# A streaming encoder step with SSD, GLA and RWKV-7 branches: weight splits in a thread, a third token-copy buffer, later transposes and gating, and new charges in the emitter

## The chip, the cores and the metric

The kernel runs on one core of a Trainium2 chip. The metric is the device time of one execution in microseconds. The engines are TensorE (PE; its weight loads are listed as PEld), VectorE (DVE), ScalarE (ACT), GpSimd (POOL) and SyncE (SP), whose queue issues nearly all DMA transfers. Each engine works off its instructions in the order in which they stand in the program; what another engine or a transfer must finish first is waited for there, with everything behind it.

## The reference

One step of a hybrid encoder layer on 544 frames (512 of a prompt and 32 of a running stream), model width 1024, and 256 memory tokens. Cut to what matters:

```python
proj = u @ w_in                      # u = RMSNorm(h); one projection for all three branches
xbc = silu(conv4(xbc)); o_ssd  = gated_rmsnorm(ssd(xs, dt, A, B, C), z)   # 16 heads x 64, state 128
glog = log_sigmoid(low_rank(u)); o_gla = head_rmsnorm(gla(q, k, v, glog)) * silu(ggate)  # 4 heads, 128 x 256
o_rwkv = (head_layernorm(rwkv7_scan(r, w, k, v, kk, a)) + bonus) * silu(rgate)           # 16 heads x 64
m = s0 * (o_ssd @ P_ssd) + s1 * (o_gla @ P_gla) + s2 * (o_rwkv @ P_rwkv)  # s = sigmoid(merge gates of u)
h = h + m @ w_out
h = h + cross_attention(RMSNorm(h), K, V)   # K, V = RMSNorm(mem) @ wk, @ wv; 4 heads x 256
y = RMSNorm(h)
```

All of it is in f32. The three recurrences are written frame by frame in the reference; the kernel evaluates them in chunks of 64 or 128 frames. In RWKV-7 a chunk needs the inverse of a unit lower-triangular 64 x 64 matrix for each head. The outputs are y, the final states of the three recurrences and the memory's K and V.

## The kernel before, in words

**Dense work.** All weights lie in DRAM as blocks of 128 output columns (128 x 1024 with the eight k-blocks side by side). A block is loaded into a tile `wraw` and split into a high part `wh` (a rounding copy on ACT) and a low part `wl` (a subtraction on DVE); the activations are split in the same way (`uh`, `ul`). A block is then multiplied in two halves of 272 frames (256 for the memory), each by 24 products into one PSUM bank `pd`: alternately uh·wh and ul·wh for the eight k-blocks, then eight times uh·wl. The page counts 4896 of these products with u and streamed blocks, and 1152 with u and blocks that stay resident (`wr`); those of the memory, the projections and the attention come on top. `wh` and `wl` have two buffers each, `wraw` two or three.

**RWKV part.** The 16 heads go as eight pairs p. For each pair, `rw_A` prepares decays and keys, stores token-major copies (tiles `tm` and t8, the latter shown as t in the profile, both from the ring `tm`; the copies go to `NK` by DMA) and forms the triangular matrices, which go to DRAM (`n_scr`). `rw_I` loads them (`nd`) and solves the diagonal 32 x 32 blocks on POOL by 31 steps of two instructions (`im`, `td`; 62 in all), then stores the inverses (`d_scr`). `rw_J` loads these into `TT`, transposes one block on DVE (x1, shown as x), and completes the inverse with two groups of small products, W and T. `rw_C` is the chain over nine chunks: a product into `pc`, the sum `R` on DVE, a product with TT, then the new state `Sb`. The solve of the next pair runs beside the chain of the current one.

**The other threads.** `start_mem` and `start_x` norm the memory and the frames at the start (column sums `pss`, then `rsm` by a logarithm and an exponential on ACT); GLA and SSD threads run beside and behind the RWKV part; `gated` and `ssd_norm` load each branch's output and gate tiles (`yt`, `gt`) back from DRAM, gate them and split them as inputs of the projections.

**What sets the order.** The whole program is written out by a small scheduler (`Sched`) when it is built. It keeps a modelled clock for each engine, and charges each instruction a modelled duration. Each part above is a Python generator, a thread with a priority; where it yields a number, it is taken up again when PE's modelled clock has advanced by that much, and `S.at(x)` is the time until x is written by the model. The dense work is the thread of lowest priority (`dense`, 9): it fills PE whenever no other thread is due, and yields after every five products. The low part of a split is a thread of priority -1, which is above all others. So a charge in the model that is changed deals out the instructions of all engines anew. On the chip the model has no part: there the fixed orders meet the real durations.

**Names and lines.** A dense product is recorded at L245, an ACT activation at L278, a DVE or POOL instruction of two tensors at L284, a DMA at L327, the transposes of TT at L1122. The high part's copy is issued in `split_w`, before the thread `low` is added; `dense` picks the next block (`more`) before a block's first product. In the model a POOL instruction in `tt` costs 2.1 ns an element and 230 ns.

Of the kernel before, what the change touches and what calls it, by code (L numbers as in the profile page):

```python
# [11 lines left out]
AF = mybir.ActivationFunctionType  # L12
# [34 lines left out]
       ("a", "v"): 145.0, ("a", "p"): 170.0, ("v", "a"): 130.0, ("v", "p"): 155.0, ("p", "v"): 70.0, ("p", "a"): 65.0,  # L47
       ("a", "q"): 150.0, ("v", "q"): 150.0, ("p", "q"): 150.0, ("v", "v"): 127.0, ("a", "a"): 153.0, ("p", "p"): 102.0}

W = dict(HOLD1=0, HOLD2=8, CALM=3000, EARLY1=1, DEPTH1=3, EARLY2=2, FAIR=1500, GRAIN=5, IS=900.0, IE=0, NQ=3000, XL=2, SG=6, PRW=800.0, R2=0.0, DE=2500.0, T2=0, FA=900.0, XM=3000.0, WARM=12, KM=1500.0)  # L50


class Cols:
# [72 lines left out]
class Sched:  # L126
# [22 lines left out]
    def run(self):  # L149
        idle = 0  # L150
        while self.threads:
# [4 lines left out]
            th = next(ready, None)  # L156
            if th is not None and th[0] >= 0 and self.n_small > W["FAIR"]:
                th = next((x for x in ready if x[0] == 9), th)
# [78 lines left out]
    def mm(self, out, lhsT, rhs, start, stop, transpose=False, shared=False):  # L237

        n = rhs.free_size()
        k, m = lhsT.partition_size(), lhsT.free_size()  # L240
        if transpose:
            self.nc.tensor.transpose(out, lhsT, rhs)  # L242
            ns = 107.0 if k > 64 else 40.0
        else:
            self.nc.tensor.matmul(out, lhsT, rhs, start=start, stop=stop, skip_group_check=shared)  # L245
            if lhsT.dtype == F32R:
                ns = n / 2.4 + 12.7
            elif m <= 64:
                ns = max(60.0, n * 0.95 + 14)
            else:  # L250
                ns = max(107.0, n * 1.67)
        small = k < 128 or m < 128
        if self.small and not small:
            ns += 150
        elif small and not self.small:
            ns += 90
        self.small = small
        self.n_small = self.n_small + ns if lhsT.dtype != F32R else 0.0
        if start:
            self.note("pe", ns, (out,), (lhsT, rhs))  # L260
        else:
            self.note("pe", ns, (), (lhsT, rhs))
            self.mark(out, 0, "pe", self.t["pe"])
# [76 lines left out]
def body(tc, I, O):  # L340
    nc = tc.nc
    S = Sched(nc)
# [17 lines left out]
    with tc.manual_schedule(), \  # L360
# [104 lines left out]
        raw, spl, splitting = {}, {}, set()  # L465
        wn = [0]
        n_late = [0]
        ahead = []
        look = {"depth": W["DEPTH1"], "early": W["EARLY1"]}

        def ready(j):
            return j.get("cond") is None or j["cond"]()
# [16 lines left out]
        def split_w(j):  # L489
            blk = j["blk"]  # L490
            if blk in spl or blk in splitting:
                return
            tag, w = raw.pop(blk)
            if "res" in j:
                h, l = (pools["res"][1].tile([128, 1088], F32R, name="wr", tag=t) for t in j["res"])
            else:
                k = wn[0] % 2
                wn[0] += 1
                h, l = (base.tile([128, 1088], F32R, name=n_, tag=f"{n_}{k}") for n_ in ("wh", "wl"))
            h, l = h[:, :1024], l[:, :1024]  # L500
            S.act(h, w, AF.Copy)
            hl = tuple(a.rearrange("p (a b) -> p a b", b=128) for a in (h, l))

            def low():
                yield S.at(h)
                S.tt(l, w, f32(h), SUB)
                free_raw[tag] = S.since(w, 1)
                done.add(f"split {blk}")
                spl[blk] = hl

            splitting.add(blk)
            S.add(low(), -1)
# [31 lines left out]
        def dense():  # L544

            nxt = []

            def more(n):
                j = take() if len(nxt) < n else None
                if j is not None:  # L550
                    nxt.append(j)

            while True:
                commit()
                more(1)
                if not nxt:
                    presplit()
                    if not ahead and "end" in done:
                        return
                    yield lambda: any(ready(j) for j in ahead) or (commit() or any(ready(j) for j in ahead)) or "end" in done  # L560
                    continue
                cur = nxt.pop(0)
                commit()
                more(1)
                presplit()
                yield lambda: cur["blk"] in spl
                h, l = spl[cur["blk"]]
                if "res" not in cur:
                    del spl[cur["blk"]]
                    splitting.discard(cur["blk"])  # L570
                x = cur["x"]
                m = cur.get("m", 128)
                hv = cur.get("hv", ((0,) + HV[0], (1,) + HV[1]))
                if "late" in cur:
                    yield lambda: n_late[0] < 3
                    n_late[0] += 1
                for hi, o, w in hv:
                    ps = pd.tile([128, 512], F32, name="pd", tag="pd")
                    yield max(S.at(h), S.since(ps, 1) - S.t["pe"])
                    c = 0  # L580
                    for kb, part in [(kb, part) for kb in range(8) for part in (0, 1)] + [(kb, 2) for kb in range(8)]:
                        if c == 16:
                            yield S.at(l)
                        a = l if part == 2 else h
                        S.mm(ps[:m, :w], a[:, kb, :m], x(kb, o, w)[part % 2], start=c == 0, stop=c == 23)
                        c += 1
                        if c % W["GRAIN"] == 0 and c < 24:
                            commit()
                            yield None
                    if hi == hv[-1][0] and W["T2"]:  # L590
                        commit()
                        more(2)
                    if "late" in cur:
                        S.add(late(cur, ps), -0.5)
                        continue
                    if "ucond" in cur:
                        yield cur["ucond"]
                    cur["use"](hi, ps)
                    done.add(f"{cur['blk']}:{hi}")
                    yield None  # L600
                done.add(cur["blk"])
# [288 lines left out]
            return a.rearrange("p (c t) -> p c t", t=64)  # L890

        HP = ((0, 288), (288, 288))
        TMB = 2

        def rw_A(p):

# [214 lines left out]
        def rw_J(p):  # L1111

            yield has(f"rwJ{p}")
            rwr = pools["rwR"][1]
            d = slot[p % NSLOT]
            nk, tt_ = d["NK"], d["TT"]
            for h in range(2):
                S.dma(out=tt_[h * 64:h * 64 + 64, :, h * 64:h * 64 + 64], in_=rows64(d_scr, h))
            yield S.at(tt_)
            x1 = rwr.tile([128, 8, 32], F32, name="x1", tag="xw")  # L1120
            for h in (0, 64):
                nc.vector.transpose(x1[h:h + 64], tt_[h:h + 64, 0:8, h:h + 32])  # L1122
                S.note("v", 340, (x1[h:h + 64],), (tt_[h:h + 64],))
            yield S.at(x1) + W["XM"]
            ps = yield from bank("pW")
            for c in range(8):
                for h in (0, 64):
                    S.mm(ps[h:h + 64, c * 32:c * 32 + 32], nk[h:h + 32, c, h // 64, h // 32, :], x1[h:h + 32, c, :], True, True)
            w = rwr.tile([128, 8, 32], F32, name="W", tag="xw")
            S.act(w.rearrange("p c j -> p (c j)"), ps[:, :256], AF.Copy)  # L1130
            yield S.at(w)
            ps = yield from bank("pT")
            for c in range(8):
                for h in (0, 64):
                    S.mm(ps[h:h + 32, c * 32:c * 32 + 32], w[h + 32:h + 64, c, :], tt_[h + 32:h + 64, c, h + 32:h + 64], True, True)
            for h in (0, 64):
                S.act(tt_[h:h + 32, 0:8, h + 32:h + 64], ps[h:h + 32, :256].rearrange("p (c t) -> p c t", t=32), AF.Copy)
            done.add(f"rwI{p}")
            yield None

        IE = "pv"[W["IE"]]
# [534 lines left out]
        def gated(br, t):  # L1676

            yield has(*[f"{dict(rwkv='rg', gla='gg')[br]}{j}" for j in range(8)])
            low = None
            for j, (yt, gt) in enumerate(gate_loads(br)):  # L1680
                yield S.at(yt, gt)
                S.stt(yt, yt, 0.5, gt, MUL, MUL)
                if low:
                    low()
                low = split_o(br, t, j, yt)
                yield S.free("v")
            low()
            done.add(f"O{br}")

        def ssd_norm(t):  # L1690
# [2 lines left out]
            yield has(*[f"z{j}" for j in range(8)])  # L1693
            ys, rr = [], []
            for j, (yt, gt) in enumerate(gate_loads("ssd")):
                yield S.at(yt, gt)
                S.stt(yt, yt, 0.5, gt, MUL, MUL)
                if j % 4 == 0:
                    sq = gp.tile([128, T], F32, name="nsq", tag="nsq")
# [423 lines left out]
```

## Time and profile before

| | before |
|---|---|
| median of 3 runs (lowest to highest) | 1303.99 us (1301.09 to 1306.32) |
| profiled execution, its own time | 1301.87 us |
| its span in the trace | 1300.1 us |
| PE busy | 1260.5 us, 97% |
| DVE busy | 838.8 us, 65% |
| ACT busy | 627.3 us, 48% |
| POOL busy | 361.6 us, 28% |
| mean granted TensorE clock | 0.99 of full speed |

The profile is of one execution. Busy time counts the instructions of an engine; PE's products are pipelined, so its busy time holds overlaps and is not work at its peak. The granted clock is a share of TensorE's full 2.4 GHz. In a timeline a row gives the start, the duration, the engine, the line, the operation with the tile that it writes and the tiles that it reads, and in brackets the idle time of the engine before it and what ended that.

### The profile page before, as it was taken

How to read it: one execution, taken by the hardware profiler on the slowest of the kernel's cores; microseconds unless marked ns; L12 is line 12 of the kernel's file. 1: busy time of each engine (PE TensorE's matmuls, PEld its weight loads, DVE VectorE, ACT ScalarE, POOL GpSimd, SP SyncE). 2: the span in 40 equal slices, each digit the busy share in tenths (PEclk: the TensorE clock that was granted, in tenths of full speed). 3: DMA queues.
4: the chain of work that ended last, by engine and by line, in shares of the span. 5: the costliest groups of instructions: out<-in, count | busy, mean ns of one | idle time of the engine just before them, and what ended most of it. 6: DMA issues, size and time to landing. Idle time of an engine off the chain costs nothing.

```text
span 1300.1 us, 27497 instructions
## 1 busy us (share of the span) xinstructions
PE 1260.5 (97%) x10848; PEld 1215.3 (93%) x10848; DVE 838.8 (65%) x1666; ACT 627.3 (48%) x1191; POOL 361.6 (28%) x706
## 2 busy tenths in 40 slices
PE   8999989999999999999999999989999999999997
PEld 8999989999998999999999999978999999999997
DVE  6857747675858586844456586877665846575543
ACT  6664534557373637444364646364444423544422
POOL 0012837375656645551001062432100000000000
PEclk8999989999999999999999999999999999999999
DMA  8644462727363635364253243343887445540302
GB/s 291 190 129 111 131 147 64 182 75 183 84 167 96 156 96 151 99 174 134 101 191 114 76 127 109 103 135 114 277 311 251 141 144 181 171 146 25 106 17 70
DMA packets 170385, 181.11 MB, mean 139 GB/s; under 512 B 100480, under 2 KB 123104, under 8 KB 170128
## 3 DMA queue, kind: packets, MB, share of 16 engines
q1 hardware_dynamic: 169824, 178.68, 45.1%
q8 instruction: 86, 1.41, 0.5%
q10 hardware_dynamic: 432, 0.67, 0.2%
q14 instruction: 43, 0.35, 0.1%
HBM read 136.27 MB, written 35.39 MB: 132 GB/s over the span
## 4 chain that ended last, share of the span: by engine, by line
PE 54%; DVE 7%; ACT 2%; issue 1%; POOL 1%; DMA 0%; POOLq 0%; DVEq 0%; ACTq 0%; SPq 0%
PE pd L245 42%; PE pc L245 2%; PE psc L245 1%; PE pov L245 1%; PE py L245 1%; PE pO L245 1%; DVE wl L284 1%; DVE acc L293 1%; PE ph L245 1%; DVE AR L284 1%; PE pT L242 1%; PE pss L245 1%; PE pS L245 0%; DVE seg L299 0%; PE pp L245 0%
## 5 line engine op out<-in xcount | busy, mean ns | idle before, releaser
L245 PE MATMUL pd<-ul,wh 128*128 128x272 f32 (+1 forms) x1632 | 434.5, 295 | 0.0
L245 PE MATMUL pd<-uh,wh 128*128 128x272 f32 (+1 forms) x1632 | 431.1, 294 | 3.1 <-ACT wh L278 2.3
L245 PEld LDWEIGHTS pd<-uh,wh 128*128 128x128 f32 (+1 forms) x1632 | 307.1, 188 | 6.9 <-ACT wh L278 2.8
L245 PEld LDWEIGHTS pd<-ul,wh 128*128 128x128 f32 (+1 forms) x1632 | 307.4, 188 | 3.0 <-issue 1.5
L245 PE MATMUL pd<-uh,wl 128*128 128x272 f32 (+1 forms) x1632 | 251.4, 291 | 0.0
L245 PEld LDWEIGHTS pd<-uh,wl 128*128 128x128 f32 (+1 forms) x1632 | 219.9, 188 | 2.7 <-issue 1.4
L284 DVE TENSOR_TENSOR wl<-wraw,wh 128x1024 fp32r<-128x1024 f32 (+1 forms) x143 | 182.2, 1277 | 29.7 <-ACT wh L278 28.2
L278 ACT ACTIVATE wh<-wraw 128x1024 fp32r<-128x1024 f32 (+1 forms) x143 | 149.3, 1047 | 44.9 <-PE pd L245 27.4
L284 POOL TENSOR_TENSOR im<-td,nd 108x84 f32<-108x84 f32 (+23 forms) x248 | 110.8, 447 | 176.4 <-DMA td<-in_eye 86.5
L245 PE MATMUL pd<-uh,wr 128*128 128x256 f32 (+1 forms) x768 | 148.6, 291 | 1.4 <-ACT uh L278 1.4
L245 PEld LDWEIGHTS pd<-uh,wr 128*128 128x128 f32 x768 | 121.0, 188 | 3.0 <-ACT uh L278 1.6
L284 POOL TENSOR_TENSOR td<-td,im 108x84 f32<-108x84 f32 (+23 forms) x248 | 117.5, 474 | 19.4
L284 POOL TENSOR_TENSOR macc<-macc,hrs 128x288 f32<-128x288 f32 x3 | 2.3, 792 | 372.6 <-DVE macc L293 372.6
L245 PE MATMUL pd<-ul,wr 128*128 128x256 f32 (+1 forms) x384 | 100.2, 292 | 0.1
L245 PEld LDWEIGHTS pd<-ul,wr 128*128 128x128 f32 x384 | 72.4, 188 | 1.0 <-issue 0.4
L278 ACT ACTIVATE lerpA<-pd,par 128x272 f32<-128x272 f32 x50 | 24.4, 487 | 71.1 <-PE pd L245 60.2
L278 ACT ACTIVATE fg<-pd 128x272 f32<-128x272 f32 x64 | 25.3, 397 | 66.2 <-PE pd L245 56.0
L293 DVE SCALAR_TENSOR_TENSOR Sb<-Sb,GC,pc 64x64 f32<-64x64 f32 x128 | 35.7, 279 | 32.3 <-PE pc L245 30.3
L278 ACT ACTIVATE NK<-pc 128x128 f32<-128x128 f32 x136 | 30.5, 275 | 46.3 <-DVE Sb L293 44.5
L278 ACT ACT_TABLE_LOAD x39 | 50.0, 1283 | 3.9 <-DVE tB L284 1.6
L293 DVE SCALAR_TENSOR_TENSOR fg<-fg,pd 128x272 f32<-128x272 f32 x48 | 20.7, 433 | 47.5 <-ACT fg L278 47.2
L278 ACT ACTIVATE fg<-pd,dpar 128x272 f32<-128x272 f32 x48 | 23.3, 486 | 51.0 <-PE pd L245 46.6
(469 smaller groups left out, 2461.1 us busy)
## 6 DMA issues: line engine op xcount, KB each, us to landing
wraw<-in_wall SPq DMA_DIRECT2D x165, 512.0 KB
g_mg<-fg SPq DMA_DIRECT2D x24, 272.0 KB
mgt<-g_mg SPq DMA_DIRECT2D x24, 272.0 KB
NK<-tm SPq DMA_DIRECT2D x96, 64.0 KB
ab<-acs_d SPq DMA_DIRECT2D x8, 512.0 KB
nd<-n_scr SPq DMA_DIRECT2D x24, 144.0 KB
n_scr<-NK SPq DMA_DIRECT2D x16, 144.0 KB
TT<-d_scr SPq DMA_DIRECT2D x16, 144.0 KB
```

The lines of the kernel that those rows point to most:

```text
L242: self.nc.tensor.transpose(out, lhsT, rhs)
L245: self.nc.tensor.matmul(out, lhsT, rhs, start=start, stop=stop, skip_group_check=shared)
L278: self.nc.scalar.activation(out=out, in_=in_, func=f, scale=scale, bias=bias)
L284: eng.tensor_tensor(out=out, in0=a, in1=b, op=op)
L293: self.nc.vector.scalar_tensor_tensor(out=out, in0=a, scalar=s, in1=b, op0=op0, op1=op1)
```

## The change

Six edits:

1. `split_w`: the ACT copy of the high part is issued inside the thread `low`, once the raw block has landed by the model; before, it was issued at once, when the block was picked.
2. `dense`: after every five products, if no next block is picked, the first block of the list `ahead` is picked when it can start and its raw weights have landed by the model (or are being split already).
3. The ring `tm` has three buffers instead of two.
4. `rw_J`: the transposes of `TT` are issued 1500 ns of modelled time later.
5. `gated` for GLA, and `ssd_norm`: each tile's gating is issued 2000 ns of modelled time later.
6. The model's charge for an f32 product with more than 64 output rows rises from max(107, 1.67 n) to max(220, 1.79 n) ns, n being its columns.

```diff
-W = dict(HOLD1=0, ..., KM=1500.0)
+W = dict(HOLD1=0, ..., KM=1500.0, TM=1500.0, GM=2000.0)
...
             else:
-                ns = max(107.0, n * 1.67)
+                ns = max(220.0, n * 1.79)
...
             h, l = h[:, :1024], l[:, :1024]
-            S.act(h, w, AF.Copy)
             hl = tuple(a.rearrange("p (a b) -> p a b", b=128) for a in (h, l))
 
             def low():
+                yield S.at(w)
+                S.act(h, w, AF.Copy)
                 yield S.at(h)
                 S.tt(l, w, f32(h), SUB)
...
                         if c % W["GRAIN"] == 0 and c < 24:
                             commit()
+                            if not nxt and any(ready(j) and (j["blk"] in spl or j["blk"] in splitting or S.at(raw[j["blk"]][1]) == 0.0) for j in ahead[:1]):
+                                more(1)
                             yield None
...
-        TMB = 2
+        TMB = 3
...
-            yield S.at(tt_)
+            yield S.at(tt_) + W["TM"]
...
-                yield S.at(yt, gt)
+                yield S.at(yt, gt) + (W["GM"] if br == "gla" else 0.0)
...
-                yield S.at(yt, gt)
+                yield S.at(yt, gt) + W["GM"]
```

At the start, on ACT: the squares (`NK`) of the memory tokens, the weights' high parts and the reciprocal norm `rsm`, in the kernel before:

```order
L278 ACTIVATE wh<-wraw 128x1024
L278 ACTIVATE NK_124<-mem 128x256 x7
L278 ACTIVATE wh<-wraw 128x1024
L278 ACTIVATE NK_124<-mem 128x256
L278 ACTIVATE wh<-wraw 128x1024 x2
L278 ACTIVATE rsm<-pss,col 128x256
L278 ACTIVATE rsm<-rsm 128x256
```

and in the changed one, the same place:

```order
L278 ACTIVATE NK_124<-mem 128x256 x2
L278 ACTIVATE wh<-wraw 128x1024
L278 ACTIVATE NK_124<-mem 128x256 x6
L278 ACTIVATE wh<-wraw 128x1024 x2
L278 ACTIVATE rsm<-pss,col 128x256
L278 ACTIVATE rsm<-rsm 128x256
L278 ACTIVATE NK_124<-AR_119 128x544
L278 ACTIVATE wh<-wraw 128x1024
```

The first block of 128 x 1024 here is the second of the program, so the fifth block's copy, which stood directly ahead of `rsm`, now stands behind it. On PE the column sums `pss` for it come after 63 dense products in the changed program and after 72 before.

On SP, the DMA queue, at the drain of the second solve and the feed of the third (`d_scr` and `TT` are the drain, `n_scr`, `nd` and `td` the feed), in the kernel before:

```order
L327 DMA d_scr<-td 36x11x32
L327 DMA d_scr<-td 36x10x32
L327 DMA d_scr<-td 36x11x32
L327 DMA TT_125<-d_scr 64x9x64 x2
L327 DMA wraw<-in_wall 128x1024
L327 DMA NK_1070<-tm 64x4x64 x4
L327 DMA g_rwkv<-fg 128x544
L327 DMA wraw<-in_wall 128x1024
L327 DMA n_scr_140<-NK_1070 64x9x64 x2
L327 DMA nd<-n_scr_140 36x32x32 x3
L327 DMA td<-in_eye 108x352
```

and in the changed one:

```order
L327 DMA w2r<-in_w2a 128x256
L327 DMA d_scr<-td 36x11x32
L327 DMA d_scr<-td 36x10x32
L327 DMA d_scr<-td 36x11x32
L327 DMA TT_125<-d_scr 64x9x64 x2
L327 DMA nd<-n_scr_140 36x32x32 x3
L327 DMA wraw<-in_wall 128x1024
L327 DMA td<-in_eye 108x352
```

The matrices of the next pair (`n_scr`) are stored before the drain now, and their load `nd` follows TT directly, with one weight block between it and `td`. At the next three drains `n_scr` follows TT directly.

On PE, in the RWKV part, the eight groups of W products (one for each pair) have 312, 302, 303, 336, 316, 341 and 322 dense products between one and the next before, 2232 in all; in the changed program 283, 207, 259, 249, 279, 289 and 306, which is 1872. The RWKV part's end comes after 3298 dense products instead of 3701.

Behind it, on PE, GLA's third head (transposes `pT`, gates `pgk`, states `pS`) beside SSD (`pxt`, `py`), in the kernel before:

```order
L245 MATMUL pA_10952<-g_qe_8886,g_ke 32x32
L242 MATMUL pxt<-con,xs_8860 32x128
L242 MATMUL pxt<-con,xs_8861 32x128
L242 MATMUL pxt<-con,xs_8862 32x128
L242 MATMUL pxt<-con,xs_8863 32x128
L242 MATMUL pT<-con,g_gl 128x128 x4
L242 MATMUL pT<-con,gvf 128x128 x8
L242 MATMUL pT<-con,gvf 32x128 x2
L242 MATMUL pT<-con,g_gl 32x128
L245 MATMUL pgk<-smt,gw_8871 128x272 x2
L245 MATMUL pS<-vt,kt 128x256
```

and in the changed one:

```order
L245 MATMUL pd<-uh,wh 128x272
L245 MATMUL pd<-ul,wh 128x272
L242 MATMUL pT<-con,g_gl 128x128 x4
L242 MATMUL pT<-con,gvf 128x128 x8
L242 MATMUL pT<-con,gvf 32x128 x2
L242 MATMUL pT<-con,g_gl 32x128
L245 MATMUL pd<-uh,wh 128x272
L245 MATMUL pd<-ul,wh 128x272
L245 MATMUL pd<-uh,wh 128x272
L245 MATMUL pd<-ul,wh 128x272
L245 MATMUL pd<-uh,wh 128x272
L245 MATMUL py<-seg,xc 64x128 x8
```

Dense products (`pd`) stand here ahead of the transposes and between them and `py` now, where none stood.

## Rows read from the trace of the kernel before

**Rows 1.** The page, busy time and share of each engine with its instructions.

```profile
PE 1260.5 (97%) x10848; PEld 1215.3 (93%) x10848; DVE 838.8 (65%) x1666; ACT 627.3 (48%) x1191; POOL 361.6 (28%) x706
```

**Rows 2.** Windows; us, then PE, PEld, DVE, ACT, POOL busy, PEclk, DMA, GB/s.

```profile
21.50:25.90 4.40, 4.38 (x24) 4.38 (x25) 3.91 (x15) 2.57 (x6) 0.00 (x0) 0.61 0.73 209
174.70:609.20 434.50, 420.48 (x4077) 404.49 (x4076) 289.51 (x610) 224.47 (x463) 236.76 (x498) 0.99 0.48 130
188.10:193.20 5.10, 4.92 (x21) 4.60 (x21) 2.63 (x7) 1.92 (x7) 4.41 (x16) 0.50 0.97 259
845.00:863.00 18.00, 14.44 (x100) 11.66 (x100) 14.27 (x38) 10.39 (x18) 2.72 (x3) 0.91 0.51 159
957.70:961.10 3.40, 3.40 (x18) 3.40 (x17) 2.13 (x3) 0.66 (x1) 0.00 (x0) 0.51 0.99 332
1040.00:1072.50 32.50, 32.50 (x262) 32.50 (x261) 16.10 (x31) 7.23 (x10) 0.00 (x0) 1.00 0.43 143
```

**Rows 3.** Timeline of ACT and PE at the start.

```profile
15.10 1.06 ACT L278 ACTIVATE wh<-wraw 128x1024 fp32r<-128x1024 f32 x1 [0.88 <-DMA wraw<-in_wall]
...
19.14 1.06 ACT L278 ACTIVATE wh<-wraw 128x1024 fp32r<-128x1024 f32 x1 [2.98 <-DMA wraw<-in_wall]
20.11 0.46 ACT L278 ACTIVATE rsm<-pss,col 128x256 f32<-128x256 f32 x1
...
21.52 0.39 PE L245 MATMUL pd<-mnh,wh 128*128 128x256 f32 x1 [2.55 <-DVE kv L284]
```

**Rows 4.** Timeline of ACT and PE around 186 us.

```profile
185.83 0.48 ACT L278 ACTIVATE t<-ptk 64x384 f32<-64x384 f32 x1 [5.64 <-DMA NK<-tm]
...
188.05 0.61 PE L245 MATMUL pn<-k,blk 128*128 128x288 f32 x1 [4.10 <-ACT k L278]
```

**Rows 5.** Timeline of DVE and PE around 355 us.

```profile
355.37 0.44 DVE L1122 STREAM_TRANSPOSE x<-TT 64x256 f32<-64x256 f32 x1 [0.95 <-DMA TT<-d_scr]
...
356.19 0.49 PE L245 MATMUL pc<-R,TT 128*128 128x128 f32 x2 [1.11 <-DVE R L284]
```

**Rows 6.** Timeline of SP's DMA queue (SPq) and POOL, 166 to 245 us.

```profile
166.60 1.30 SPq L327 DMA_DIRECT2D d_scr<-td  x3
...
223.97 1.28 SPq L327 DMA_DIRECT2D d_scr<-td  x3
227.01 1.42 SPq L327 DMA_DIRECT2D TT<-d_scr  x2
...
234.80 1.28 SPq L327 DMA_DIRECT2D n_scr<-NK  x2
238.25 2.41 SPq L327 DMA_DIRECT2D nd<-n_scr  x3
...
244.77 0.44 POOL L284 TENSOR_TENSOR im<-td,nd 108x31 f32<-108x31 f32 x1 [20.82 <-DMA g_rwkv<-fg]
```

**Rows 7.** Windows of POOL (busy, PEclk, DMA, GB/s): td's instructions alone, then all.

```profile
306.00:347.30 41.30, 30.06 (x62) 1.00 0.39 115
564.10:590.70 26.60, 21.72 (x62) 1.00 0.47 144
...
306.00:347.30 41.30, 36.34 (x72) 1.00 0.39 115
```

**Rows 8.** Tile wh: DVE's low-part subtraction, lowest/median/highest ns, first to last start.

```profile
L284 DVE TENSOR_TENSOR wl<-wraw,wh x143: 684/1220/2449, 10.3 to 1097.0; 128x1024 fp32r<-128x1024 f32 x141, 128x512 fp32r<-128x512 f32 x2
```

**Rows 9.** PE's waits (total us, times, longest), then the timeline around 956 us.

```profile
PE pd L245 <- ACT wh L278: 2.3, 3, 1.5
...
955.12 1.05 ACT L278 ACTIVATE wh<-wraw 128x1024 fp32r<-128x1024 f32 x1
...
956.27 0.49 PE L245 MATMUL pd<-o__11911,wh 128*128 128x272 f32 x2 [2.19 <-issue]
```

More of the change, by code (lines that the diff above doesn't have):

```diff
@@ L48 @@
        ("a", "q"): 150.0, ("v", "q"): 150.0, ("p", "q"): 150.0, ("v", "v"): 127.0, ("a", "a"): 153.0, ("p", "p"): 102.0}
-W = dict(HOLD1=0, HOLD2=8, CALM=3000, EARLY1=1, DEPTH1=3, EARLY2=2, FAIR=1500, GRAIN=5, IS=900.0, IE=0, NQ=3000, XL=2, SG=6, PRW=800.0, R2=0.0, DE=2500.0, T2=0, FA=900.0, XM=3000.0, WARM=12, KM=1500.0)
+W = dict(HOLD1=0, HOLD2=8, CALM=3000, EARLY1=1, DEPTH1=3, EARLY2=2, FAIR=1500, GRAIN=5, IS=900.0, IE=0, NQ=3000, XL=2, SG=6, PRW=800.0, R2=0.0, DE=2500.0, T2=0, FA=900.0, XM=3000.0, WARM=12, KM=1500.0, TM=1500.0, GM=2000.0)
 class Cols:
```

## The prediction

> **What bounds the kernel now.** I read the page's first part, then the stretches by windows, then the timelines of ScalarE (ACT), VectorE (DVE), GpSimd (POOL) and of the SyncE DMA queue (SP) where TensorE (PE) waits. PE is busy 1260.5 of 1300.1 us [rows 1]: 39.6 us idle is all that a new order can win directly. A stretch of dense weight products alone runs 262 in 32.50 us, 0.124 us each, at the full granted clock [rows 2]; none of these edits makes a product shorter. The second loss is the clock: after four of the longer waits the granted clock stands at half for some microseconds (0.61 over 21.5 to 25.9, 0.50 over 188.1 to 193.2, 0.91 over the 18 us from 845, 0.51 over 957.7 to 961.1 [rows 2]), at 1.2 instead of 2.4 GHz. So I price waits, and the half-clock stretches behind the long ones.
>
> **The change part by part.** No product, copy or transfer is added or taken away; the edits move instructions. The sum is made against the profiled execution, 1301.87 us (span 1300.1 and 1.8 around it), which lies 2.1 us under the median of the runs, 1303.99.
>
> *High parts in a thread: the start.* ACT stands 2.98 us for the fifth weight block's landing, with the logarithm for rsm queued behind that copy; rsm frees the PSUM banks, and PE waits 2.55 us at 21.52 [rows 3]. In the changed order that copy stands behind both rsm instructions, and PE issues its column sum (pss) after 63 dense products instead of 72. What is ahead of rsm then is the wh copy at 15.10 us, over long before. rsm can start about 2 us earlier; I leave 0.5 us of the wait, a gain of 2.0. The slow clock behind it costs 24 products 4.40 us where 24 x 0.124 is 3.0: another 1.4. Bounds: 0 (the bank still late) to 4.
>
> *Third tm buffer.* With two, the small copy t takes the buffer whose stores were just issued: ACT stands 5.64 us for them, the next pair's square and high part k stand behind, and PE waits 4.10 us [rows 4]. With three buffers t takes that of the pair's first copy, stored long before. The wait goes, and with it the 5.1 us at half clock, worth 2.5. If the cover is thinner than I think, 0.
>
> *More time at transposes (TM).* The transposes of TT stand in DVE ahead of the chain's R or state. One stood 0.95 us, and R behind it held PE 1.11 us [rows 5]. Starting them 1.5 us later by the emitter's clock would hide waits of this size, if the distance to TT stayed.
>
> *It does not stay.* The inverse of each head pair is solved on POOL by 62 products, fed and drained through DRAM by SP. In the trace SP issues the drain d_scr at 166.60 and 223.97, 57.4 us apart [rows 6]. The chain has these steps: d_scr to the end of the TT issues 4.5 us (223.97 to 228.43); n_scr to nd 3.45; nd to the first product 6.5 (238.25 to 244.77) [rows 6]. A solve takes 41.3 us, in which POOL is busy 36.34, of this 30.06 with its own 62 [rows 7]; without the 6.3 of other work it is 35.0.
> Before, n_scr came 7.8 us after TT [rows 6], for want of other work in the queue; the changed SP order puts nd straight behind TT for the third pair, and n_scr straight behind it for the next ones. So solves follow each other more closely, but PE's order draws closer still. Between the first and last of the eight groups of W products PE issues 2232 dense products before and 1872 after; the rest of the dense work moves behind the RWKV part. PE's time per pair is then its dense count at 0.124 plus the small products: 420.48 us busy in that stretch [rows 2], less 2.5 for the slow clock and 2232 x 0.124 = 276.8, leaves 141.2, or 20.2 for each of seven pairs. The counts after are 283, 207, 259, 249, 279, 289, 306, so PE needs 55.3, 45.9, 52.3, 51.1, 54.8, 56.0 and 58.1 us.
> The chain needs, with the steps above: for the third pair (207) 4.5 + 0.4 (one weight issue) + 6.5 + 35.0 + 5.0 (five of the ten other instructions remain inside; 3.1 to 6.3) = 51.4; for the fourth 4.5 + 3.45 + 0.8 + 6.5 + 35.0 + 5.0 = 55.2; for the fifth, with all ten inside, 56.1; for the sixth about 56.3. The others come out even. PE is short by 5.5, 2.9, 5.0 and 1.5: 14.9 us. As the transposes stand in DVE directly ahead of R or of the state in the changed order too, nearly all of it is a wait of PE; one microsecond of slack leaves 14, and I add 2 for ordinary waits. Before, PE was idle 434.50 - 420.48 = 14.0 us here, the 4.1 of t among it. RWKV therefore goes from 14 to 16 idle, and from 2.5 to about 5 of slow clock behind two or three waits of 4 us and more: +4.5. Bounds: 4 us idle (the chain hidden; -12.5) and the chain at the 57.4 us that rows show (+21, below).
>
> A rule of the Trainium skill speaks against the change here. In the trace the last solve, with DVE quieter, takes its 62 products in 26.6 us, 21.72 busy, against 30.06 elsewhere [rows 7], and the low-part subtraction wl takes 1220 ns in the median but up to 2449 [rows 8]. The page "SBUF — State Buffer", section "SBUF: two separate sides", says that DVE and GpSimd share one port pair as an exclusive lock, which a DVE operation with two SBUF inputs contends for. By it, DVE work packed some 12% closer would lengthen each solve by about 12% of the 8.3 us difference, 1 us, and the sum would be some 4 us worse. By the row alone it stays at 35.0, which I take.
>
> *Split in the middle of a block.* At 953.9 the first projection block became ready after its predecessor was under way; its high part came behind the last tanh, at 955.12, and PE waited 2.19 us [rows 9]. With the new test the next block is taken between two groups of five products. The three waits for wh add 2.3 us [rows 9], one of them 0.4 I leave; together 4.1 go, and 1.2 of slow clock (18 products in 3.40 us, 2.2 at full clock [rows 2]). Bounds 0 to 5.3.
>
> *Dense work left for the GLA and SSD part.* From 845 to 863 PE is busy 14.44 of 18 us [rows 2]: the order has no dense product between the third head's A and its output products. After, ten or so stand ahead of the transposes and a few in each gap, since RWKV used up fewer of them. I take 3.0 of the 3.6 idle and 1.4 of the clock. Bounds 0 to 5.
>
> *At nothing:* GM (2 us more for each of 8 tiles, two passes: GLA's gating has the first projection's eight blocks, 8 x 48 x 0.124 = 48 us, over it; uncovered it costs 16 us a pass) and the new charges of f32 products, whose effect is the counts above.
>
> The sum: -3.4 (start) +4.5 (RWKV) -5.3 (split) -4.4 (GLA) = -8.6. 1301.87 - 8.6 = 1293.3, and 2.1 for the median: 1295.
>
> **The rivals.**
> A, *the chain stays hidden*: its steps overlap more than I count. For it: before, a mean of 60 us between drains contained idle queue time. Against: the 51.4 us holds only steps that follow one another. RWKV then keeps 4 us idle: -10 -2.5 instead of +4.5, in all -25.6: 1276 + 2 = 1278.
> B, *the chain paces at 57.4 us*, as in the only two drains shown; the place is the transposes ahead of R in DVE. For it: a d_scr that waits in SP holds the stores and weights behind it; only two weight buffers serve this part. Against: the 7.8 us gap before n_scr goes. PE is short 2.1, 11.5, 5.1, 6.3, 2.6, 1.4 = 29: 30 idle instead of 14, and 5 more of clock, +21: in all +7.9, 1309.8 + 2.1 = 1312, slower than before. It decides from about 26 us idle there, where the gains are spent.
> C, *the order is dealt anew*: start, split and GLA gain nothing because other waits of the same size appear; only +4.5 stays: 1306 + 2 = 1308. For it: every engine's order differs; against: the three places look better in the order itself.
>
> **How the numbers follow.** Forecast 0.45, between 1289 and 1301; A 0.27; B 0.14; C 0.14. 1295 is the forecast's own. The range of 8 in 10 reaches from A's value to just under B's, 1278 to 1311. No change is within 0.5% (6.5 us; about what a measurement of this kernel can tell): 1297.5 to 1310.5. Faster: A and six tenths of the forecast, 0.55; same: the forecast's rest and most of C, 0.29; slower: B and little else, 0.16.
>
> **What would show it.** Right: no PE wait on kv near 20 us; no ACT wait of microseconds before t; the third and fifth group of W products, or R just ahead, late by 4 to 6 us with DVE's transposes waiting for TT; drains 51 to 56 us apart; dense products between A and py; wh of the first projection ahead of the last tanh. Wrong: if the transposes never wait (A), if the drains stay 57 us apart (B), or if PE's idle time outside RWKV doesn't fall by some 9 us (C).

## The result and the profile after

The changed kernel takes 1312.98 us (median of 5 runs, 1310.56 to 1315.53) against 1303.99 before: ratio 1.0083, 95% interval 1.0061 to 1.0104. It is 0.8% slower; the forecast was 1295, in a range of 1278 to 1311. The profiled execution took 1311.71 us, with a span of 1309.9. All ratios are of fast executions; of the runs below this leaves out one, of 2433.43 us, with the third buffer alone.

PE's busy time and its share, on the page of the changed kernel, answer to [rows 1]:

```profile
PE 1266.4 (97%) x10848; PEld 1221.0 (93%) x10848; DVE 843.3 (64%) x1666; ACT 621.0 (47%) x1187; POOL 358.8 (27%) x706
```

PE does the same 10848 instructions and is busy 5.9 us longer: a sign of the slow clock. The stretch of the RWKV part, from the first to the last group of W products, and its five half-clock stretches, in windows with the columns of [rows 2]:

```profile
172.40:578.30 405.90, 381.77 (x3697) 365.44 (x3698) 278.09 (x592) 199.93 (x419) 232.06 (x490) 0.97 0.47 124
176.70:187.00 10.30, 6.83 (x83) 6.39 (x84) 4.98 (x8) 4.54 (x9) 3.88 (x6) 0.50 0.66 172
303.00:309.90 6.90, 6.12 (x28) 6.15 (x28) 4.47 (x8) 3.70 (x8) 6.12 (x12) 0.51 0.44 140
395.20:398.60 3.40, 3.37 (x15) 3.37 (x16) 1.50 (x5) 0.00 (x0) 0.00 (x0) 0.50 0.44 95
439.60:443.00 3.40, 3.40 (x16) 3.40 (x17) 3.33 (x7) 0.38 (x3) 3.18 (x5) 0.50 0.21 82
518.10:521.50 3.40, 3.40 (x16) 3.40 (x17) 1.52 (x5) 0.45 (x2) 0.00 (x0) 0.50 0.90 263
```

In this way every kernel below is measured: the time of this stretch less 0.124 us for each dense product in it (the *overhead*: small products, idle time, slow clock), and the same for what lies ahead and behind. The *slow clock* is half of the time that PE is busy at half clock: here half of 6.83 + 6.12 + 3.37 + 3.40 + 3.40, or 11.6 us.

| | before | changed |
|---|---|---|
| ahead of the first W product, overhead | 31.9 | 33.3 |
| RWKV stretch: us, dense products | 435.5, 2232 | 405.9, 1872 |
| its overhead | 158.7 | 173.8 |
| its idle PE time, slow clock | 14.0, 2.5 | 24.1, 11.6 |
| behind it, overhead | 160.4 | 153.8 |
| ahead: idle PE time, slow clock | 6.2, 3.4 | 6.2, 1.7 |
| behind, to PE's last product: idle PE time, slow clock | 11.6, 3.4 | 5.6, 1.7 |

By overhead RWKV costs 15.1 us more, the start 1.4 more, and the rest 6.6 less: +9.9. But the work of the stretches is not the same: 48 small products that stand between the first and last W products before stand ahead of them (12) or behind them (36) in the changed kernel. Idle time and slow clock alone are free of that: RWKV +19.2, the start -1.7, the rest -7.7, in all +9.8, which is the difference of the two spans. The start's +1.4 is those 12 products less the 1.7, and no more than the scatter between runs: without the split within a block (un_mid, below) all compute engines have the same order up to there, and the first W product starts at 170.58 us instead of 172.43.

### The profile page after: what moved, and what is told of

Same layout as the page of the kernel before. It is cut to its first block, busy times and chain, and to the rows that moved or that the text cites. A ratio compares the mean times of both kernels' runs of the same rounds, so it can differ in the third digit from the quotient of the medians.

```text
span 1309.9 us, 27531 instructions
## 1 busy us (share of the span) xinstructions
PE 1266.4 (97%) x10848; PEld 1221.0 (93%) x10848; DVE 843.3 (64%) x1666; ACT 621.0 (47%) x1187; POOL 358.8 (27%) x706
## 4 chain that ended last, share of the span: by engine, by line
PE 60%; DVE 3%; ACT 1%; POOL 1%; DMA 1%; issue 1%; SPq 0%; POOLq 0%; DVEq 0%; ACTq 0%
PE pd L245 47%; PE pc L245 2%; PE psc L245 1%; PE py L245 1%; PE pO L245 1%; PE pov L245 1%; PE ph L245 1%; PE pS L245 1%; PE pss L245 1%; DVE wl L284 1%; PE pT L242 1%; DVE acc L293 0%; PE pA L245 0%; SPq L327 0%; PE pl L245 0%
## 5 line engine op out<-in xcount | busy, mean ns | idle before, releaser
L245 PE MATMUL pd<-ul,wh 128*128 128x272 f32 (+1 forms) x1632 | 441.0, 298 | 0.0
L245 PEld LDWEIGHTS pd<-ul,wh 128*128 128x128 f32 (+1 forms) x1632 | 310.7, 190 | 4.2 <-issue 2.4
L284 DVE TENSOR_TENSOR wl<-wraw,wh 128x1024 fp32r<-128x1024 f32 (+1 forms) x143 | 180.5, 1265 | 57.9 <-ACT wh L278 57.4
L284 POOL TENSOR_TENSOR im<-td,nd 108x84 f32<-108x84 f32 (+23 forms) x248 | 108.1, 436 | 97.7 <-DMA NK<-tm 26.9
L293 DVE SCALAR_TENSOR_TENSOR Sb<-Sb,GC,pc 64x64 f32<-64x64 f32 x128 | 35.7, 279 | 31.9 <-PE pc L245 29.5
L245 PE MATMUL pc<-NK 128*128 128x64 f32 x288 | 43.8, 276 | 5.0 <-DVE NK L1190 4.9
L245 PEld LDWEIGHTS pc<-NK 128*128 128x128 f32 x288 | 39.4, 196 | 8.0 <-DVE NK L1190 4.9
```

What stands on the lines that cost most here:

```text
L284: eng.tensor_tensor(out=out, in0=a, in1=b, op=op)
L293: self.nc.vector.scalar_tensor_tensor(out=out, in0=a, scalar=s, in1=b, op0=op0, op1=op1)
```

## Where PE waits in the changed kernel

The waits of PE by what ended them, longest sums first (us in total, times, longest):

```profile
PE pc L245 <- DVE R L284: 6.7, 6, 3.6
PE pT L245 <- ACT W L278: 5.8, 1, 5.8
PE pd L245 <- DVE wl L284: 5.2, 6, 2.5
PE pc L245 <- DVE NK L1190: 4.9, 5, 2.8
PE pc L245 <- DMA Sb<-in_s_rwkv: 4.7, 3, 3.4
PE pd L245 <- ACT wh L278: 4.6, 4, 2.1
```

Three kinds of these are new in size. First, at the end of the first solve, the timeline of SP's queue, ACT and PE:

```profile
163.44 1.31 SPq L327 DMA_DIRECT2D d_scr<-td  x3
166.42 1.28 SPq L327 DMA_DIRECT2D TT<-d_scr  x2
167.81 3.02 SPq L327 DMA_DIRECT2D nd<-n_scr  x3
170.88 1.43 SPq L327 DMA_DIRECT2D b_scr<-rs  x1
172.36 2.61 SPq L327 DMA_DIRECT2D NK<-tm  x4
175.07 0.55 SPq L327 DMA_DIRECT2D wraw<-in_wall  x1
...
178.79 1.06 ACT L278 ACTIVATE wh<-wraw 128x1024 fp32r<-128x1024 f32 x1 [6.85 <-DMA wraw<-in_wall]
179.75 0.37 ACT L278 ACTIVATE W<-pW 128x256 f32<-128x256 f32 x1
...
180.17 1.07 PE L245 MATMUL pT<-TT,W 32*32 32x32 f32 x32 [5.81 <-ACT W L278]
```

SP stands until the solve is drained at 163.44; a weight block is issued only 11.6 us later, behind TT, nd and a group of stores. ACT waits 6.85 us for it, with W behind, and PE waits 5.81 us for W. The wait of [rows 4] is gone, and this one has come in its place.

Second, at the fifth drain, SP, DVE and PE:

```profile
386.16 1.29 SPq L327 DMA_DIRECT2D d_scr<-td  x3
387.54 2.67 SPq L327 DMA_DIRECT2D NK<-tm  x4
390.38 1.27 SPq L327 DMA_DIRECT2D TT<-d_scr  x2
...
393.25 0.44 DVE L1125 STREAM_TRANSPOSE x<-TT 64x256 f32<-64x256 f32 x1 [2.56 <-DMA TT<-d_scr]
394.88 0.29 DVE L284 TENSOR_TENSOR R<-pc,NK 128x128 f32<-128x128 f32 x1
...
395.23 0.79 PE L245 MATMUL pc<-R,TT 128*128 128x128 f32 x2 [3.60 <-DVE R L284]
```

This is the predicted wait, [rows 5] three times as long. At 518 it is the product behind NK that waits for the same cause, DVE's transposes standing for TT:

```profile
516.08 0.44 DVE L1125 STREAM_TRANSPOSE x<-TT 64x256 f32<-64x256 f32 x1 [2.44 <-DMA TT<-d_scr]
...
518.01 0.86 PE L245 MATMUL pc<-NK 128*128 128x64 f32 x3 [2.77 <-DVE NK L1190]
```

Third, an initial state that is loaded last in the queue:

```profile
298.83 1.20 SPq L327 DMA_DIRECT2D Sb<-in_s_rwkv  x2
...
303.78 0.55 PE L245 MATMUL pc<-Sb,AR 128*128 128x128 f32 x1 [3.44 <-DMA Sb<-in_s_rwkv]
```

At the start the predicted gain is there: rsm at 18.28 instead of 20.11, and the wait for kv is 0.46 us instead of 2.55 [rows 3].

```profile
18.28 0.47 ACT L278 ACTIVATE rsm<-pss,col 128x256 f32<-128x256 f32 x1 [2.12 <-PE pss L245]
...
19.71 0.39 PE L245 MATMUL pd<-mnh,wh 128*128 128x256 f32 x1 [0.46 <-DVE kv L284]
```

## The experiments

Ratios are to the kernel before in the same series. *Chain*: the solve on POOL with its drain and feed through SP sets the pace of the RWKV part. *Queue*: SP's stores of the token copies hold back weights. *Order*: any new order loses as much somewhere.

**Single edits undone: TMB = 2; the old charge; TM = 0; the ACT copy issued at once; no split within a block.**

```diff
-        TMB = 3
+        TMB = 2
```


> All of the change but the third tm buffer. It deals 278, 317, 341, 297, 250, 294 and 330 dense products between the groups of W products (2107; the changed kernel 1872, before 2232). Chain theory (PE waits where it needs less than the some 57 us that the drains show; PE's need is 0.124 us a dense product and 20.2 us of small ones): 54.7, 59.5, 62.5, 57.0, 51.2, 56.7 and 61.1 us, so only the first and the fifth are short, by 2 and 6 us: 1301 to 1306. Queue theory (the third buffer lets the stores of three tm tiles pile up in SP ahead of weights and TT, and that is what was lost): the pile-up is gone, the t wait of some 5 us on ACT is back: 1300 to 1305. Order theory (any newly dealt order loses some 10 us at random places): 1308 to 1316.


```diff
-                ns = max(220.0, n * 1.79)
+                ns = max(107.0, n * 1.67)
```


> All of the change but the new charges of f32 products. It deals 288, 240, 288, 288, 336, 302 and 322 dense products (2064). Chain theory: PE's need is 55.9, 50.0, 55.9, 55.9, 61.9, 57.6 and 60.1 us, so the second is short by 7 us and three by 1: 1302 to 1307. Queue theory: the third buffer is still there, so 1309 to 1315. Order theory: 1308 to 1316.


```diff
-TM=1500.0
+TM=0.0
```


> All of the change but the 1500 ns at the transposes (TM = 0). It deals 293, 235, 259, 274, 331, 264 and 341 dense products (1997). Chain theory: PE's need is 56.5, 49.3, 52.3, 54.2, 61.2, 52.9 and 62.5 us, short of 57 by 0.5, 7.7, 4.7, 2.8, 0, 4.1 and 0, in all 20: 1307 to 1313, with PE waits at R behind the transposes in the second, third and sixth interval. Queue theory: 1309 to 1315, with waits for weights and Sb behind NK<-tm stores. Order theory: 1308 to 1316, anywhere.


```diff
+            S.act(h, w, AF.Copy)          # in split_w, ahead of low()
             def low():
-                yield S.at(w)
-                S.act(h, w, AF.Copy)
```


> All of the change but the high parts' thread: the ACT copy is issued at once again. It deals 293, 269, 293, 292, 288, 298 and 288 dense products (2021). Chain theory: PE's need is 56.5, 53.6, 56.5, 56.4, 55.9, 57.2 and 55.9 us, nearly level, short of 57 by 7 in all, while the wait at the start is back: 0.996 to 1.003 of before. If it is the copies in the thread that come late for W and R in the RWKV part, it is better than that, 0.990 to 0.996. Order theory: 1.003 to 1.012.


```diff
-                            if not nxt and any(...): more(1)
```


> All of the change but the split in the middle of a block. The RWKV part's dense products are those of the changed kernel (283, 207, 259, 249, 279, 289, 306). If the split gives what the prediction gave it, 5.3 us behind the RWKV part, the time is 4 to 6 us over the changed kernel, 1.011 to 1.013 of before, with waits for wh of 1 to 2 us at the first projection back. If it gives nothing, 1.006 to 1.010.

| undone | ratio (95%) | dense | RWKV overhead | idle, slow clock there | behind |
|---|---|---|---|---|---|
| (none) | 1.0083 (1.0061 to 1.0104) | 1872 | 173.8 | 24.1, 11.6 | 153.8 |
| tm buffer | 0.9980 (0.9960 to 1.0000) | 2107 | 166.6 | 17.7, 6.6 | 151.3 |
| charges | 0.9936 (0.9915 to 0.9957) | 2064 | 161.0 | 18.0, 7.7 | 152.1 |
| TM | 1.0134 (1.0083 to 1.0184) | 1997 | 175.7 | 24.0, 14.5 | 156.0 |
| high parts | 1.0080 (1.0059 to 1.0101) | 2021 | 177.8 | 26.7, 9.7 | 152.6 |
| split | 1.0091 (1.0065 to 1.0117) | 1872 | 174.9 | 26.6, 8.8 | 152.5 |

Without the new charges the other five edits gain 0.64%, without the third buffer 0.2%, at the edge of the noise. TM's worth isn't shown: without it one R waits 6.7 us behind the transposes, but its interval overlaps that of the whole change. The thread of the high parts costs nothing that shows: without it PE has a more level need, for which chain gave 0.996 to 1.003, and yet RWKV is no better, mostly by one wait of 7.4 us at 184, where ACT stood 13.2 us for a gate store's transfer; 1.0080 lies in the range of order. Without the charges the time is below every range given, without TM above. So the counts alone, from which chain worked out its numbers, don't decide. The split within a block gives nothing behind RWKV: 152.5 without it, 153.8 with it.

**Shorter solves, in the order of either kernel.**

```diff
             for s in range(31):
...
+                if 8 <= s < 24:
+                    S.note("p", ...)      # charged, not issued; both instructions
+                else: ...                 # as before
```


> The changed kernel with 32 of each solve's 62 POOL products left out (steps 8 to 23) but still charged by the emitter, so that every engine has the same order as in the changed kernel; only the solves are shorter, by some 25 of 40 us. Chain theory: the transposes find TT landed; PE's idle time between the first and last W products falls from 24.1 to under 10 us, the clock's loss there from 13.7 to under 5, and the time to 1290 to 1300. Queue theory: the stores stand in SP as before, idle time there stays above 16 us and the time at 1303 or more. Order theory: 1303 or more.

> The kernel before with 32 of each solve's 62 POOL products left out (steps 8 to 23) but still charged by the emitter, every engine's order being that of before: the control for the same cut in the changed kernel, which took 26 us out of its RWKV part. Chain theory: before had enough dense work between drains, so the cut finds little to take: from the first to the last W products 434.5 us falls by 4 to 10, idle time from 14 to 7 to 10; 0.992 to 0.997 of before. If shorter solves free any order of so much (less traffic of POOL beside DVE), it falls by over 15: below 0.988.

Measured 0.9855 (0.9827 to 0.9883) and 0.9902 (0.9878 to 0.9925). The RWKV stretch, first of the changed order, then of the order before:

```profile
171.30:551.30 380.00, 372.76 (x3700) 357.14 (x3700) 272.72 (x592) 199.35 (x419) 125.16 (x266) 1.00 0.48 129
```
```profile
174.00:596.30 422.30, 417.66 (x4107) 402.95 (x4108) 282.26 (x608) 224.22 (x463) 128.92 (x274) 1.00 0.50 134
```

25.9 us go from the changed kernel and 13.2 from the one before, more than expected there; the overheads are then 147.9 and 145.6. Idle time and slow clock there fall from 35.7 to 8.9 us in the changed order and from 16.5 to 4.6 in the one before, so of the 19.2 us between the two kernels 4.3 are left: the changed order is nearly as good as the old one where the solves are short. Little moved behind RWKV (154.0 and 160.8).

**Without the stores of the token copies.** From the second pair on, the transfers of the two sets of tiles are charged but not issued, and two memsets on POOL ahead of the first solve stand in for the data; beside it the third buffer alone, in the kernel before.

```diff
+        if in_.name not in self.skip:
             getattr(self.nc, q).dma_start(out=out, in_=in_)
...
+                if p:
+                    S.skip.add(tm.name)   # and t8.name
```


> The changed kernel with the stores of the token-major copies (NK<-tm and NK<-t, 16 transfers a pair) left out from the second pair on, though still charged by the emitter: the order of all else is that of the changed kernel, but SP issues some 10 us less for each pair; two memsets on POOL before the first solve stand in for the data. Chain theory (the solve's 40 us and the drain and feed steps set the pace): RWKV from the first to the last W products falls little, 405.9 to 396 or more. Queue theory (weights, Sb and gate stores stand in SP behind these stores): the wait of 5.8 us at the second W products and those for Sb go, RWKV to 380 to 392, as in the run with the solves cut. If both hold in series (SP stands for the drain, and the stores stand behind it), something between: 388 to 398.


```diff
-        TMB = 2                           # only_tmb: the kernel before with this alone
+        TMB = 3
```


> The kernel before with the third tm buffer alone. It deals 298, 302, 299, 296, 317, 299 and 306 dense products (2117), level, with a need of 57 to 59.5 us each. Chain theory: the t wait of 4.1 us and its half clock go, the drains are just in time: 0.993 to 0.998 of before. Queue theory (the buffer lets stores pile up ahead of weights): 1.000 to 1.008.

> The same left out of the kernel before with the third buffer alone, which took 436.0 us from the first to the last W products, with a wait of 7.5 us at 184 while ACT stood 13.3 us for a gate store behind these stores. Queue theory: that wait goes and RWKV falls by 12 to 20 us, the time to 0.990 to 1.000 of before. Chain theory: RWKV falls by under 6, the time stays at 1.004 or more.

Measured 1.0034 (1.0016 to 1.0053), 1.0107 (1.0066 to 1.0147) and 1.0053 (1.0030 to 1.0075). The stores' going takes 7.0 us out of the changed kernel's stretch:

```profile
171.70:570.60 398.90, 378.37 (x3701) 360.82 (x3700) 277.17 (x592) 200.02 (x419) 232.91 (x490) 0.98 0.39 112
```

and 7.6 out of that with the third buffer alone (436.0 to 428.4). Both are less than queue gave. The first is within chain's range and 0.9 us outside the one for both in series; the second is within chain's time, though over its 6 us. Without the stores Sb's waits are gone from the changed kernel, and of the 5.81 us at the second W products PE still waits 4.08:

```profile
177.69 0.53 PE L246 MATMUL pT<-TT,W 32*32 32x32 f32 x12 [4.08 <-ACT W L279]
```

So the stores are the smaller part of that wait, and the late drain with TT and nd behind it the larger (with the solves cut it is gone). A wait of 4.5 us for a copy on POOL, at 321, is new in this run. Chain's miss is only_tmb, to which it gave a gain. Its largest wait, 7.5 us, shows why; ACT stands for a gate store behind the burst:

```profile
179.13 2.61 SPq L327 DMA_DIRECT2D NK<-tm  x4
181.78 0.56 SPq L327 DMA_DIRECT2D td<-in_eye  x1
182.44 2.57 SPq L327 DMA_DIRECT2D NK<-tm  x4
...
188.34 0.38 SPq L327 DMA_DIRECT2D g_rwkv<-fg  x1
...
191.14 0.40 ACT L278 ACTIVATE fg<-pd 128x272 f32<-128x272 f32 x1 [13.31 <-DMA g_rwkv<-fg]
```

**The charges alone, and the three edits that leave RWKV's counts.** The new charges in the kernel before; and high parts, split and GM without the other three.

```diff
-                ns = max(107.0, n * 1.67)   # only_mm: the kernel before with this alone
+                ns = max(220.0, n * 1.79)
```


> The kernel before with the new charges of f32 products alone. It deals 278, 317, 322, 321, 307, 336 and 288 dense products (2169; before 2232). Chain theory: PE's need is 54.7, 59.5, 60.1, 60.0, 58.3, 61.9 and 55.9 us, over the chain's 57 but for 2 and 1 us, so the charges do little harm where the other edits don't tighten the order too: 0.998 to 1.004 of before. If the charges are bad by themselves, as much as they cost in the changed kernel (1.5%): 1.008 or more.


```diff
-max(220.0, n * 1.79)  TMB = 3  TM=1500.0     # late3: the changed kernel with these taken back
+max(107.0, n * 1.67)  TMB = 2  TM=0.0
```


> Three of the six edits: the high parts in a thread, the split in the middle of a block, and the gating 2000 ns later. The dense products between the groups of W products are those of the kernel before (2232 in all), so the RWKV part keeps its room. Chain theory: RWKV costs what it did before, and what the edits gain outside it is kept: some 3 us at the start, 4 to 5 at the blocks' borders, 0 to 4 in the GLA part, so 0.991 to 0.997 of before. Order theory: as much is lost at new places, 0.998 to 1.008.

Measured 1.0044 (1.0029 to 1.0059), just over the chain's bound, and 0.9971 (0.9955 to 0.9986), at the edge of it. In late3 the start has 2.3 us less overhead and the end 5.7 less, but RWKV 6.5 more in the profiled execution, which at 1300.32 us is 4.7 over the median of its runs: the slow clock there is 9.7 instead of 2.5, the idle time unchanged (13.8). The charges cost 0.4% alone and 1.5% on top of the other five.

**A truer charge for the solve.**

```diff
-        ... n * 2.1 + 230, (out,), (a, b))
+        ... n * 2.1 + 330, (out,), (a, b))
```


> The whole change, and in the emitter POOL's charge for a product raised from 2.1 n + 230 to 2.1 n + 330 ns, which makes a solve some 35 us there, as recorded, instead of 29. It deals 245, 246, 301, 279, 312, 292 and 303 dense products (1978; the changed kernel 1872). Chain theory: PE's need by 0.124 and 20.2 us is 50.6, 50.7, 57.5, 54.8, 58.9, 56.4 and 57.8 us, short of 57 by 6.4, 6.3, 0, 2.2, 0, 0.6 and 0, 15 in all instead of 27: 0.997 to 1.003 of before, 5 to 12 us under the changed kernel. Order theory: no better than the changed kernel, 1.003 to 1.012.

> The kernel before with POOL's charge alone raised to 2.1 n + 330. It deals 312, 331, 331, 331, 351, 331 and 346 dense products (2333), a need of 59 to 64 us, over the chain's 57. Chain theory: before was over it already in all seven, so the charge gives little here: 0.995 to 1.001 of before. If the charge helps whatever the order (it gave 1.5% in the changed kernel): 0.990 or less.

Measured 0.9934 (0.9909 to 0.9959) for the whole change with it, 1.5% below the change; RWKV overhead 155.4, idle 12.8. In the kernel before it alone gave 1.0083 (1.0056 to 1.0110), worse than either theory said. There RWKV did improve, overhead 153.9 and idle 9.2, but it used 2333 dense products, and left the GLA and SSD part behind it fewer: overhead behind 176.2 instead of 160.4. Its window from 845 to 925, of which PE is busy 67.31, and its longest wait:

```profile
845.00:925.00 80.00, 67.31 (x538) 59.42 (x536) 53.52 (x124) 36.15 (x62) 22.25 (x24) 0.89 0.36 113
```
```profile
914.40 0.91 PE L245 MATMUL py<-seg,xc 128*64 128x128 f32 x6 [4.85 <-DVE seg L284]
```

In the changed kernel PE is busy all of the same 80 us. So dense products are a stock: too few in RWKV and the chain shows, too many and GLA starves.

**A version that beats both.** On top of pool330 the next pair's Sb is loaded in the fourth chunk of the running chain instead of ahead of its own, and then also two tm buffers.

```diff
-            for i in range(2):
+            for i in range(2 if p == 0 else 0):
...
+                if c == 3 and p < 7:
+                    S.flush(Sb[2].name)
+                    for i in range(2):
+                        S.dma(out=Sb[2][64 * i:64 * i + 64, i], in_=I["s0_rwkv"][64 * i:64 * i + 64, p + 1])
```


> pool330 with the initial state Sb of the next pair loaded in the fourth chunk of the current chain instead of behind the last copies of its own pair. It deals 245, 254, 279, 283, 288, 307 and 303 dense products (1959). The three waits of PE for that load, 3.8 us in pool330, go, and 0 to 2 us of half clock: 0.989 to 0.993 of before. If another wait of the chain stands behind each (R, TT), no better than pool330: 0.992 to 0.996.


```diff
-        TMB = 3
+        TMB = 2
```


> pool330_sb with two tm buffers again. It deals 283, 303, 331, 336, 293, 293 and 345 dense products (2184), a need of 55 to 63 us. Chain theory: the pace is met, and the t wait of some 4 us on PE is back: 0.990 to 0.997 of before. Queue theory: with two buffers no weight stands behind three tiles' stores, so it is better than pool330_sb: 0.984 to 0.991.

Measured 0.9922 (0.9897 to 0.9947), 1289.84 us against 1299.82 in that series, and 0.9925 (0.9901 to 0.9950). The waits for Sb are gone; idle time in RWKV is 10.5 us, overhead 155.1:

```profile
183.10:581.10 398.00, 387.53 (x3822) 370.16 (x3821) 274.39 (x582) 205.68 (x430) 224.18 (x486) 0.99 0.46 127
```

Against pool330 the intervals overlap, so the load's own worth isn't shown. Nor is the third buffer's, once the pace is met.

## Why the prediction was wrong

It is 18.4 us short in the profiled execution (1293.3 forecast, 1311.71 measured): by idle time and slow clock 14.7 in RWKV, 1.7 at the start, 2.0 behind.

*RWKV, +4.5 forecast, +19.2 measured: the step that failed.* The mechanism was right in kind: the counts fall, the drains come late, PE waits behind the transposes, and with short solves most of it goes. The pace was nearly right too, up to the last. Between drains it gave 51.4, 55.2, 56.1 and 56.3 us from the third pair on, and SP's queue shows 52.6, 55.6, 57.6 and 60.5; the third interval's two ends and its first product are

```profile
272.98 1.30 SPq L327 DMA_DIRECT2D d_scr<-td  x3
...
289.86 0.69 POOL L284 TENSOR_TENSOR im<-td,nd 108x31 f32<-108x31 f32 x1 [9.00 <-DMA NK<-tm]
...
328.53 1.29 SPq L327 DMA_DIRECT2D d_scr<-td  x3
```

What failed are two terms of the sum. The first is the idle time: 14 us behind the transposes, then "I add 2 for ordinary waits". Idle time is 24.1 instead of 16, and of it only 7.6 stand behind the transposes (1.20, 3.60 and 2.77); the ordinary waits are 16.5. Before, 9.9 us of such stood in the stretch (14.0 less the 4.1 of t), and the sum gave no reason for their going. W behind a weight (5.8) and Sb (4.7) are 10.5 of them, both behind what a drain and the stores hold up in SP's queue, a path that the sum left out. The second is the clock: "about 5 of slow clock behind two or three waits of 4 us and more" became five half-clock stretches, 27.4 us long, which cost 11.6. They begin in or just behind waits of 5.81, 3.44, 3.60, 0.71 and 2.77 us, only one of them over 4. Of the 14.7 us, 8.1 are the idle time and 6.6 the clock.

*Rival B* (1312) came nearest in time, and what was said for it is seen: "a d_scr that waits in SP holds the stores and weights behind it". Its pace of 57.4 was a little slow for the first intervals; the seven have a mean of 56.7. That its sum fits to 1 us is luck in part: it had 30 us idle, the waits at the transposes, and 5 more of clock, where 24.1 and 9.1 were measured, and its own sign, about 26 us idle, is not reached. It had 0.14; the row that spoke for it, two drains 57.4 apart [rows 6], weighed less with me than the sum of steps, and it should have been the other way round. *Rival A* fell, with 24.1 us idle instead of 4. *Rival C*, order alone, fell with cut_after, and by the 9.4 us that start, split and GLA did give.

*Third tm buffer*: "the wait goes" failed. With it PE waits 5.8 us a little earlier for W; without it (un_tmb) 2.6 us for k, and 2.4 once more at 377. The bound of 0 for thin cover was too kind; alone it costs 1.07%.

*Start, -3.4 forecast, -1.7 measured.* The wait for kv went as said, and its half clock. But the idle time is given back by 172 us, most of it by a wait of 2.07 us for a high part at 139.77; un_wh, with the kv wait back, has no more overhead there (32.9), so the gain isn't clear of scatter.

*Split and GLA, -9.7 forecast, -7.7 measured.* At the first projection PE no longer waits (before 2.19 us [rows 9]), but un_mid shows the same without the split: it was the new order, not that edit. The GLA starvation went, since 2294 dense products stand between the last group of W products and the first projection instead of 1905; late3, with the old counts, keeps it (waits of 1.30 and 1.23 us near 851 and 863).

*The charges, "at nothing"*, put down to the counts alone, are the edit that costs most: with them 1872 dense products stand in RWKV, without them 2064. They make the small products dearer in the model, and so leave fewer dense products between two solves, which the model believes shorter than they are. It charges a solve 22.6 us by 2.1 n + 230, the sum over its 62 products; the trace has 28.92 of them busy within 38.60 us in the third interval. That the old charges, too low for products of 64 columns, had covered for it is an explanation that fits pool330, where the solve's charge alone gives the 1.5% back; that this is the way it works isn't shown by itself, as the order changes everywhere.

*The port lock.* By the Trainium skill ("SBUF — State Buffer", "SBUF: two separate sides"), DVE and GpSimd take a shared port pair as an exclusive lock, by which denser DVE work would lengthen the solves. No run here shows that: the same solve products are busy 28.92 us in the window 289.9 to 328.5, with DVE busy for 78% of it, against 30.06 in [rows 7], with DVE busy for 71%.

Left open: GM was not tried by itself, and how the half-clock stretches follow from the waits is seen only in their places.

## What to carry to other kernels

When a modelled duration is corrected in a scheduler, look for the one that it was compensating: the new charge was nearer the trace for products of 64 columns, and cost 1.5% until the solve's charge went the same way. Off-path work that feeds a chain is judged by the interval between its drains against the cover in between, and in an in-order DMA queue everything behind a drain that waits is priced too. The slow clock behind the waits is priced as well: here it was 9.1 of the 19.2 us. Cover is a stock: what is put into one stage is missing in another.

## What was unexpected in the hardware

At the end of a wait of 2.9 us on PE in late3 (up to 293.97) the granted clock fell to half at 293.0 and stayed there to 310.1, 17 us in which PE was busy 16.13; with the 7.5 us wait in only_tmb (up to 192.06) it was 186.5 to 196.8. The stores of 64 KB, in 64 rows, take SP's queue 0.65 us each (2.61 for four at 172.36 in the changed kernel), where the weight block of 512 KB behind them takes 0.55: here the bytes don't set it. With the eight stores that come next the queue spends 7.7 us on twelve. From start to start of two in a row at full clock, f32 products of 128 rows with 64 columns (pc<-NK) take 165 to 272 ns on PE in the trace of the changed kernel (one 443), half of them over 204, and those with 128 columns (pO) 221: with half the columns the time falls little.
